# Own-phase keys of two attention groups in one 128-column segment, the division moved from the gate to the probabilities, and the value split regrouped

## The chip, the cores and the metric

The kernel runs on one core of one Trainium2 chip. The metric is the device time of one execution in microseconds (us). The engines are TensorE (PE, with its weight loads listed apart as PEld), VectorE (DVE), ScalarE (ACT), GpSimd (POOL) and SyncE (SP), which issues most of the transfers.

## The reference, cut to what matters

Two layers over 256 tokens of width 2048, in float32. Layer 0, where the change lies, is attention with three head groups of 16 heads each; a query of a group with dilation d attends to itself and to the tokens at multiples of d behind it, within a window.

```python
ATT_GROUPS = ((128, 1), (512, 4), (2048, 16))     # (window, dilation)
for g, (window, dilation) in enumerate(ATT_GROUPS):
    q = _head_rms(qkv[:, :, g, 0], q_gain[g]); k = _head_rms(qkv[:, :, g, 1], k_gain[g]); v = qkv[:, :, g, 2]
    o, lse = _dilated_window_attention(q, k, v, table, window, dilation)   # s = q.k/sqrt(128) + bias, softmax, p.v
w = jax.nn.softmax(jnp.stack(lses, axis=0), axis=0)
o = jnp.sum(w[..., None] * jnp.stack(outs, axis=0), axis=0)
y = o.reshape(B, S, ATT_WIDTH) * jax.nn.silu(z)
return y @ w_out
```

Weighing the three groups by their softmax denominators is the same as one softmax over the keys of all three. Layer 1 is a convolution module; the change doesn't touch it.

## The kernel before

**Tokens.** They are ordered by phase (token number modulo 4), 64 of each phase, in two blocks of 128 (`b`): block 0 holds phases 0 and 1, block 1 phases 2 and 3. Groups 1 and 2 (dilations 4 and 16) only ever look at keys of the query's own phase; group 0 looks at all.

**Precision.** Each float32 operand of a product is split into a high and a low part of a narrower format (`hi`, `lo`), and a product is three matmuls: high by high, low by high, high by low. The high part is a cast on ACT; the low part is a subtraction on DVE or POOL.

**The loop.** The program is one hand-ordered loop over 480 weight chunks of 512 KB. At step n PE multiplies chunk n (`project`: 12 matmuls of 512 columns), then chunk n+3 is fetched on SP's queue and split (`stage`: `hi` on ACT, `lo` on DVE, or on POOL in the output projection), and then the functions that `at(n, ...)` has put down for step n are written out. Those put down with `when=soon` come ahead of `stage`. Each engine runs its own instructions strictly in the order written. Steps 0 to 319 are the attention's input projection: eight sets of two heads, five column groups of eight steps each: (q,k) of groups 0, 1, 2, then the values of groups 0 and 1, then the values of group 2 with the gate `z`. The products of a column group lie in two of four PSUM banks (`acc`) that are used in turn. From step 320 comes the output projection (`wo`), which takes all four banks at once at its first step.

**A set's attention** runs among the steps of the next set, in four units (two heads by two token blocks): `scores` on PE, `softmax` (bias adds and maximum on DVE, exponential on ACT), `weigh` (reciprocal of the sum, which before scales the gate `zs`), `turn` (transposes of the probabilities on PE), `split` (high part on ACT, low on DVE). After both units of a head `values` runs on PE into bank `o`; `gated` and `y_split` make the output's parts. An ordinary set has three steps between units, the last set, whose attention runs among the output projection, two.

**What the steps touch.** Scores of a unit are 512 columns wide: 256 keys of group 0, then 128 keys of the query's block for each of groups 1 and 2, half of which are of the other phase and are masked by the bias. The bias is made at the start (`bias_rows`) in rows of eight segments of 128 per phase, held in DRAM (`btab`) and fetched per head. `v_split` (L359) splits the value banks, `z_take` (L374) copies the gate out of the last bank. `make_identity` gives `ident` for transposes; `r0` is the per-token norm, `r0h` half of it.

Of the kernel before, what the change touches and what calls it, by code (L numbers as in the profile page):

```python
# [11 lines left out]
F32 = mybir.dt.float32  # L12
F32R = mybir.dt.float32r
# [24 lines left out]
V_HEAD = V_BIN  # L38


@with_exitstack
def hybrid_kernel(ctx: ExitStack, tc: tile.TileContext, x_perm, x_tok, x_nat, vecs, rel, onehot, maskrow,
# [104 lines left out]
    xh = bpool.tile([P, KT, S], F32R, tag="xh", name="xh")  # L147
    xl = bpool.tile([P, KT, S], F32R, tag="xl", name="xl")
# [10 lines left out]
    r0 = cpool.tile([P, 2], F32, name="r0")  # L159
    r0h = cpool.tile([P, 2], F32, name="r0h")  # L160
# [3 lines left out]
    def x_split(k, xr):  # L164
        g0 = vec[:, V_G0 + k:V_G0 + k + 1]
        if k == 0:
            nc.vector.tensor_scalar(xh[:, k, :], xr, g0, None, op0=ALU.mult)
        else:
            nc.scalar.activation(xh[:, k, :], xr, AF.Copy, scale=g0)
        nc.vector.scalar_tensor_tensor(xl[:, k, :], xr, g0, xh[:, k, :].bitcast(F32), op0=ALU.mult, op1=ALU.subtract)  # L170
# [59 lines left out]


    btab = dram.tile([NH, 4096], F32, name="btab")
    brow = {}

    def bias_load(part):

        if part == 0:
            brow["rb"] = apool.tile([N_BUCKETS, NG * NH], F32, name="rb")
            nc.sync.dma_start(brow["rb"], rel)
            brow["oh"] = bpool.tile([N_BUCKETS, 4096], F32, tag="yl", name="oh")  # L240
            nc.sync.dma_start(brow["oh"], onehot)
        else:
            brow["row"] = bpool.tile([NH, 4096], F32, tag="yh", name="row")
            nc.sync.dma_start(brow["row"], bass.AP(tensor=maskrow.tensor, offset=maskrow.offset, ap=[[0, NH], [1, 4096]]))

    def bias_split(f):
        if f == 0:
            brow["hi"] = apool.tile([N_BUCKETS, NG * NH], F32R, name="rb_hi")
            brow["lo"] = apool.tile([N_BUCKETS, NG * NH], F32R, name="rb_lo")
            nc.scalar.copy(brow["hi"], brow["rb"])  # L250
            nc.vector.tensor_tensor(brow["lo"], brow["rb"], brow["hi"].bitcast(F32), op=ALU.subtract)
        brow["oh_r"] = apool.tile([N_BUCKETS, 1024], F32R, tag="pp", name=f"oh_r{f}", bufs=1)
        nc.scalar.copy(brow["oh_r"], brow["oh"][:, f * 1024:(f + 1) * 1024])

    def bias_rows(f, half):
        ps = t_tile(f"ps_b{f}_{half}")
        for g, c0, c1 in (((0, 0, 512),), ((1, 0, 256), (2, 256, 512)))[half]:
            for i, part in enumerate(("hi", "lo")):
                nc.tensor.matmul(ps[:NH, c0:c1], lhsT=brow[part][:, g * NH:(g + 1) * NH],
                                 rhs=brow["oh_r"][:, half * 512 + c0:half * 512 + c1], start=i == 0, stop=i == 1)  # L260
        row = brow["row"][:, f * 1024 + half * 512:f * 1024 + (half + 1) * 512]
        nc.vector.tensor_tensor(row, ps[:NH, :], row, op=ALU.add)

    def bias_store(f):
        sl = slice(f * 1024, (f + 1) * 1024)
        nc.scalar.dma_start(btab[:, sl], brow["row"][:, sl])

    for i in range(2):
        at(11 + i, bias_load, i)
# [8 lines left out]
    def load_bias(head):  # L278

        bt = apool.tile([P, 2, 512], F32, tag="bt", name=f"bt{head}", bufs=2)  # L280
        base = btab[:, :]
        for f in range(4):
            src = bass.AP(tensor=base.tensor, offset=base.offset + head * 4096 + f * 1024,
                          ap=[[1, 64], [128, 8], [1, 64]])
            p0 = (f % 2) * 64
            nc.sync.dma_start(bt[p0:p0 + 64, f // 2, :].rearrange("p (s i) -> p s i", s=8), src)
# [4 lines left out]
    def project(n):  # L291
# [9 lines left out]
        for i in range(2):  # L301
            k = kc * 2 + i
            wh, wl = hi[:, i * 512:(i + 1) * 512], lo[:, i * 512:(i + 1) * 512]
            for b, p in order:
                sl = slice(b * P, (b + 1) * P)
                nc.tensor.matmul(acc[b], lhsT=(xl if p == 1 else xh)[:, k, sl], rhs=wl if p == 2 else wh,  # L306
# [52 lines left out]
    def v_split(hs, part, width):  # L359
        acc = acc_a[hs * CG + 3 + part]  # L360
        out_ = []
# [641 lines left out]
```

## Time and profile before

| | |
|---|---|
| median of 3 runs | 1446.06 us (1444.73 to 1446.16) |
| the profiled execution, own time | 1443.28 us |
| its span, first to last instruction | 1441.5 us |
| PE busy | 1431.2 us, 99% |
| weight loads busy | 1186.3 us, 82% |
| DVE busy | 968.8 us, 67% |
| ACT busy | 720.3 us, 50% |
| POOL busy | 381.4 us, 26% |
| transfers | 272.09 MB, mean 189 GB/s |

Busy time is the union of an engine's instructions. Matmul records overlap: a 512-column matmul is listed with some 0.39 us, and the next starts 0.23 us after it, so on PE the distance from start to start is read. A row of the order of time gives the start, the length, the engine, the line, what is written and read, the shape, and in brackets idle time of the engine before it with what ended it.

### The profile page before, as it was taken

The page shows a single profiled execution, that of the slowest core. Times are in us where ns is not written, and L with a number is a line of the kernel's source. Part 1 is how long each engine was busy: PE and PEld are TensorE (multiplying, and loading weights), DVE is VectorE, ACT ScalarE, POOL GpSimd, SP SyncE. Part 2 cuts the span into 40 slices and gives each one's busy share as a digit, 9 for nine tenths or more (in the row PEclk, how much of TensorE's full clock was granted, in tenths as well). Part 3 has the DMA queues.
Part 4 walks back from the last instruction along what each step waited for, and adds up shares of the span by engine and source line. Part 5 has one row for each costly group of instructions (what it writes and reads, how often), then busy time and mean ns, then how long its engine had stood idle before and what let it go on. Part 6 is the DMA issues. An engine that isn't in the chain of part 4 may idle for free.

```text
span 1441.5 us, 18597 instructions
## 1 busy us (share of the span) xinstructions
PE 1431.2 (99%) x6730; PEld 1186.3 (82%) x6730; DVE 968.8 (67%) x1537; ACT 720.3 (50%) x999; POOL 381.4 (26%) x279
## 2 busy tenths in 40 slices
PE   9999999999999999999999999999999999999998
PEld 7778888888888888888888888888888888888777
DVE  6665765765676576576567657656668999988542
ACT  7544545454455454445445545544554445545642
POOL 0210120010011002001001100207104878787455
PEclk9999999999999999999999999999999999999999
DMA  9775558568557655755855765666665656665463
GB/s 353 234 196 193 157 176 220 160 174 218 169 165 193 197 166 178 208 171 165 220 172 163 194 199 162 179 170 235 193 208 183 185 179 191 177 192 171 146 205 132
DMA packets 108092, 272.09 MB, mean 189 GB/s; under 512 B 42224, under 2 KB 42736, under 8 KB 107824
## 3 DMA queue, kind: packets, MB, share of 16 engines
q1 hardware_dynamic: 107296, 270.23, 63.2%
q8 instruction: 53, 0.87, 0.3%
q10 hardware_dynamic: 704, 0.68, 0.2%
q14 instruction: 39, 0.32, 0.1%
HBM read 268.51 MB, written 2.36 MB: 188 GB/s over the span
## 4 chain that ended last, share of the span: by engine, by line
PE 95%; DVE 2%; ACT 1%; DMA 1%; issue 1%; POOL 1%; SPq 0%; DVEq 0%; ACTq 0%; POOLq 0%
PE acc L306 61%; PE b L536 6%; PE b L537 6%; PE b L538 6%; PE wo L536 2%; PE wo L538 2%; PE wo L537 2%; PE psq L343 1%; PE vo L538 1%; PE vo L536 1%; PE vo L537 1%; PE pt L430 1%; PE pg L697 1%; ACT hi L122 1%; PE o L457 1%
## 5 line engine op out<-in xcount | busy, mean ns | idle before, releaser
L122 ACT CAST hi<-raw 128x1024 fp32r<-128x1024 f32 x477 | 496.5, 1050 | 308.0 <-PE acc L306 177.0
L125 DVE TENSOR_TENSOR lo<-raw,hi 128x1024 fp32r<-128x1024 f32 x360 | 446.4, 1241 | 274.8 <-ACT hi L122 268.1
L306 PE MATMUL acc<-hi,xh 128*128 128x512 f32 x1280 | 505.4, 397 | 0.0
L306 PE MATMUL acc<-lo,xh 128*128 128x512 f32 x1280 | 497.3, 391 | 0.0
L306 PE MATMUL acc<-hi,xl 128*128 128x512 f32 x1280 | 495.6, 389 | 0.0
L125 POOL TENSOR_TENSOR lo<-raw,hi 128x1024 fp32r<-128x1024 f32 x117 | 283.6, 2459 | 151.4 <-ACT hi L122 98.5
L306 PEld LDWEIGHTS acc<-lo,xh 128*128 128x128 f32 x1280 | 240.0, 188 | 52.3 <-DVE lo L132 0.6
L306 PEld LDWEIGHTS acc<-hi,xh 128*128 128x128 f32 x1280 | 240.2, 188 | 49.2 <-issue 2.8
L306 PEld LDWEIGHTS acc<-hi,xl 128*128 128x128 f32 x1280 | 240.6, 188 | 47.0 <-DVE xl L170 0.4
L144 POOL TENSOR_SCALAR rq<-ss 128x4 f32<-128x4 f32 x48 | 10.3, 215 | 786.1 <-DVE ss L325 784.2
L750 DVE SCALAR_TENSOR_TENSOR c<-u,vec,c 128x256 f32<-128x256 f32 x480 | 190.5, 481 | 0.0
L536 PE MATMUL b<-hi,hh 128*128 128x512 f32 x384 | 151.0, 393 | 0.0
L538 PE MATMUL b<-lo,hh 128*128 128x512 f32 x384 | 149.7, 390 | 0.0
L537 PE MATMUL b<-hi,hl 128*128 128x512 f32 x384 | 149.5, 389 | 0.0
L538 PEld LDWEIGHTS b<-lo,hh 128*128 128x128 f32 x384 | 72.1, 188 | 15.1
L537 PEld LDWEIGHTS b<-hi,hl 128*128 128x128 f32 x384 | 72.2, 188 | 14.5
L536 PEld LDWEIGHTS b<-hi,hh 128*128 128x128 f32 x384 | 72.1, 188 | 14.4
L419 ACT ACTIVATE pr<-sc,m 128x512 f32<-128x512 f32 x32 | 23.2, 724 | 100.4 <-DVE m L417 100.4
L356 DVE TENSOR_TENSOR qk<-psq,qk 128x256 fp32r<-128x256 f32 x48 | 20.3, 422 | 51.1 <-ACT qk L355 51.1
L538 PE MATMUL vo<-lo,bh 128*128 128x512 f32 (+1 forms) x130 | 50.6, 389 | 1.5 <-POOL lo L125 1.5
L536 PE MATMUL wo<-hi,yh 128*128 128x512 f32 x128 | 51.3, 401 | 0.0
L536 PE MATMUL vo<-hi,bh 128*128 128x512 f32 (+1 forms) x130 | 50.4, 388 | 0.0
(145 smaller groups left out, 1299.2 us busy)
## 6 DMA issues: line engine op xcount, KB each, us to landing
raw<-w_in SPq DMA_DIRECT2D x319, 512.0 KB, 4.3
raw<-v_in SPq DMA_DIRECT2D x96, 512.0 KB, 4.3
raw<-w_out SPq DMA_DIRECT2D x32, 512.0 KB, 4.2
raw<-v_out SPq DMA_DIRECT2D x32, 512.0 KB, 4.3
bt<-btab SPq DMA_DIRECT2D x64, 128.0 KB, 6.0
x_tok<-x_tok SPq DMA_DIRECT2D x4, 512.0 KB, 8.5
x<-x_nat SPq DMA_DIRECT2D x4, 512.0 KB, 7.4
xr<-x_perm SPq DMA_DIRECT2D x7, 256.0 KB, 4.6
```

Of the source, the lines that this page charges most:

```text
L122: nc.scalar.copy(hi, raw)
L125: low_engine(n).tensor_tensor(lo, raw, hi.bitcast(F32), op=ALU.subtract)
L306: nc.tensor.matmul(acc[b], lhsT=(xl if p == 1 else xh)[:, k, sl], rhs=wl if p == 2 else wh, start=k == 0 and p == 0, stop=k == KT - 1 and ...
L343: nc.tensor.transpose(ps[:, c, :], qn[:, c, :], ident)
L356: nc.vector.tensor_tensor(ql, ps[:, 0:2], qh.bitcast(F32), op=ALU.subtract)
L419: nc.scalar.activation(u.pr.rearrange("p a b -> p (a b)"), sc, AF.Exp, bias=u.m[:, 1:2], accum_out=u.m[:, 2:3])
L430: nc.tensor.transpose(u.pt[:, c, :], u.pr[:, c, :], ident)
L457: nc.tensor.matmul(po[:, 2 * b * P:2 * (b + 1) * P], lhsT=vh[:, cs], rhs=pp[:, 2 + i, 2 * b:2 * b + 2, :], start=False, stop=False, skip_g ...
L536: nc.tensor.matmul(acc, lhsT=xh_, rhs=wh, start=first, stop=False, skip_group_check=part)
L537: nc.tensor.matmul(acc, lhsT=xl_, rhs=wh, start=False, stop=False, skip_group_check=part)
L538: nc.tensor.matmul(acc, lhsT=xh_, rhs=wl, start=False, stop=last, skip_group_check=part)
L750: nc.vector.scalar_tensor_tensor(c[j], u, w, c[j], op0=ALU.mult, op1=ALU.add)
```

## The change

Own-phase keys of groups 1 and 2 now share one 128-column segment: for a query of phase f, 64 columns of one group and 64 of the other, so a unit's scores are 384 columns wide and no own-phase column is masked for phase. The score matmuls stay as they were; the four halves are picked out of their result by DVE adds of 64 partitions by 64 columns. Which group comes first in the segment depends on the phase.

- `turn` transposes three blocks of 128 and no longer four; `split` takes 384 columns.
- `values`: the own-phase products have 128 and 64 moving columns instead of 256 and 128. Their weights `w` hold 64 tokens of one group and 64 of the other, so that `v_split` writes them in halves of 64 partitions. For this the fifth column group (values of group 2, and the gate) is projected with the tokens turned by 64: `xh` and `xl` get 64 tokens more at their end (`turn_norm`, two POOL copies), `rs` holds the norms in turned order (five small transfers), and `z_turn` and `z_put` turn the gate back, with two copies.
- `split_scaled` writes the high parts of a bank (ACT) ahead of its low parts (DVE).
- `weigh` multiplies the probabilities by the reciprocal on ACT; the gate isn't scaled any more.
- In the last set `v_split` and `z_take` of the last bank pair come ahead of `stage` (`when=soon`).
- The bias: 33 rows by 3072 columns, with a 33rd row for the masked places in place of a mask row that was added; the bias tiles have 384 columns.

```diff
+    def turn_norm():
+
+        nc.sync.dma_start(rs[:64], rr[64:])
+        for c in range(4):
+            nc.sync.dma_start(rs[64:, c:c + 1], rr[:64, c ^ 1:(c ^ 1) + 1])
+        for x in (xh, xl):
+            nc.gpsimd.tensor_copy(x[:, :, S:], x[:, :, :64])
+
+    at(20, turn_norm)
...
     def bias_rows(f, half):
         ps = t_tile(f"ps_b{f}_{half}")
-        for g, c0, c1 in (((0, 0, 512),), ((1, 0, 256), (2, 256, 512)))[half]:
+        h0 = half * 512
+        pieces = [(0, 0, 512)] if half == 0 else [(1 + f % 2, 0, P), (2 - f % 2, P, 2 * P)]
+        for g, c0, c1 in pieces:
             for i, part in enumerate(("hi", "lo")):
                 nc.tensor.matmul(ps[:NH, c0:c1], lhsT=brow[part][:, g * NH:(g + 1) * NH],
-                                 rhs=brow["oh_r"][:, half * 512 + c0:half * 512 + c1], start=i == 0, stop=i == 1)
...
+                t0 = b * P + 64 * (cg % CG == 4)
+                tokens = (xl if p == 1 else xh)[:, k, t0:t0 + P]
+                nc.tensor.matmul(acc[b], lhsT=tokens, rhs=wl if p == 2 else wh,
...
+    def split_scaled(pieces):
+
+        for hi, lo, src, r in pieces:
+            nc.scalar.activation(hi, src, AF.Copy, scale=r)
+        for hi, lo, src, r in pieces:
+            nc.vector.scalar_tensor_tensor(lo, src, r, hi.bitcast(F32), op0=ALU.mult, op1=ALU.subtract)
+
+    def v_split(hs, part):
...
+        for b in range(2):
+            pieces = []
+            if part == 0:
+                pieces.append((*sets[hs].v0[b], acc[b][:, :S], r0[:, b:b + 1]))
+            c0, r = ((S, r0), (0, rs))[part]
+            for i in range(2):
+                ps = slice(i * 64, (i + 1) * 64)
+                w = sets[hs].w[b ^ (part & i)]
+                pieces.append((*[x[ps, i ^ part, :] for x in w], acc[b][ps, c0:c0 + S], r[ps, b:b + 1]))
+            split_scaled(pieces)
...
+        for g in range(2):
+            for p in range(2):
+                ps, c = slice(p * 64, (p + 1) * 64), p ^ g
+                nc.vector.tensor_tensor(s6[ps, 4 + c], u.py[ps, g, 0, ps], bias[ps, 4 + c], op=ALU.add)
+                nc.vector.tensor_tensor(s6[ps, 4 + c], s6[ps, 4 + c], u.py[ps, g, 1, ps], op=ALU.add)
...
         nc.vector.reciprocal(u.m[:, 3:4], u.m[:, 2:3])
-        zs = u.set.zs[u.b][:, u.h * P:(u.h + 1) * P]
-        nc.vector.tensor_scalar(zs, zs, u.m[:, 3:4], None, op0=ALU.mult)
+        nc.scalar.activation(u.pr, u.pr, AF.Copy, scale=u.m[:, 3:4])
...
-        for c in range(4):
+        for c in range(3):
             nc.tensor.transpose(u.pt[:, c, :], u.pr[:, c, :], ident)
...
+            wh, wl = st.w[b]
+            for f_ in range(2):
+                qs = slice(f_ * 64, (f_ + 1) * 64)
+                nc.tensor.matmul(po4[:, 2 * b:2 * b + 2, f_, :], lhsT=wh[:, f_, cs], rhs=pp[:, 2, 2 * b:2 * b + 2, qs],
                                  start=False, stop=False, skip_group_check=True)
-                nc.tensor.matmul(po[:, q0:q0 + P], lhsT=vl[:, cs], rhs=pp[:, 2 + i, 1 + b, :],
-                                 start=False, stop=i == 1, skip_group_check=True)
+                nc.tensor.matmul(po4[:, 1 + b, f_, :], lhsT=wl[:, f_, cs], rhs=pp[:, 2, 1 + b, qs],
+                                 start=False, stop=True, skip_group_check=True)
...
-        at(e + 1 - last, v_split, hs, 1, 256)
-        at(e + 1 - last, z_take, hs)
+        at(e + 1 - last, v_split, hs, 1, when=soon if last else steps)
+        at(e + 1 - last, z_take, hs, when=soon if last else steps)
```

How the change moves instructions stands at three places. In the rows below a name is that of the tile written, then `<-` and the tiles read, then the shape written; a number at a name's end tells buffers apart.

ACT, between the last step of the input projection and the first exponential of the last set, before (`vh`: high values of a bank, `zs`: the gate):

```order
L365 ACTIVATE vh_1_0_8407<-acc_0_8243,r_82 128x256
L365 ACTIVATE vh_1_1_8411<-acc_1_8244,r_82 128x256
L379 ACTIVATE zs_0_8415<-acc_0_8243,r0h 128x256
L379 ACTIVATE zs_1_8417<-acc_1_8244,r0h 128x256
L122 CAST hi_8436<-raw_8435 128x1024
L122 CAST hi_8464<-raw_8463 128x1024
L419 ACTIVATE pr_0_8475,m_0_8470<-sc_0_8469,m_0_8470 128x512
```

The same place now (`wh`: high values in halves of 64 partitions):

```order
L378 ACTIVATE wh_0_8509<-acc_0_8487,rs 64x256
L378 ACTIVATE wh_1_8513<-acc_0_8487,rs 64x256
L378 ACTIVATE wh_1_8513<-acc_1_8488,rs 64x256
L378 ACTIVATE wh_0_8509<-acc_1_8488,rs 64x256
L407 ACTIVATE zs_0_8665<-acc_0_8487,rs 128x256
L407 ACTIVATE zs_1_8667<-acc_1_8488,rs 128x256
L123 CAST hi_8670<-raw_8669 128x1024
L123 CAST hi_8692<-raw_8691 128x1024
L123 CAST hi_8720<-raw_8719 128x1024
L448 ACTIVATE pr_0_8737,m_0_8726<-sc_0_8725,m_0_8726 128x384
```

Two high parts stand ahead of the gate copies instead of one per bank, and one more cast (that of chunk 322, which stood ahead of this place) stands behind them.

DVE, the same place up to the first unit's gate scaling, before (`vl`: low values, `sc`: scores with bias, `m`: maximum, sum and reciprocal):

```order
L366 SCALAR_TENSOR_TENSOR vl_1_0_8408<-acc_0_8243,r_82,vh_1_0_8407 128x256
L366 SCALAR_TENSOR_TENSOR vl_1_1_8412<-acc_1_8244,r_82,vh_1_1_8411 128x256
L412 TENSOR_TENSOR sc_0_8469<-s_0_8441,bt_8307 128x256
L413 TENSOR_TENSOR sc_0_8469<-sy_0_8442,bt_8307 128x256
L416 TENSOR_TENSOR sc_0_8469<-sc_0_8469,sy_0_8442 128x256
L417 TENSOR_REDUCE m_0_8470<-sc_0_8469 128x1
L387 SCALAR_TENSOR_TENSOR zs_0_8415<-e_0_8496,zs_0_8415 128x256
L423 RECIPROCAL m_0_8470<-m_0_8470 128x1
L425 TENSOR_SCALAR zs_0_8415<-zs_0_8415,m_0_8470 128x128
```

The same place now, where the pair L444, L445 stands four times in all:

```order
L380 SCALAR_TENSOR_TENSOR wl_0_8510<-acc_0_8487,rs,wh_0_8509 64x256
L380 SCALAR_TENSOR_TENSOR wl_1_8514<-acc_0_8487,rs,wh_1_8513 64x256
L380 SCALAR_TENSOR_TENSOR wl_1_8514<-acc_1_8488,rs,wh_1_8513 64x256
L380 SCALAR_TENSOR_TENSOR wl_0_8510<-acc_1_8488,rs,wh_0_8509 64x256
L126 TENSOR_TENSOR lo_8671<-raw_8669,hi_8670 128x1024
L439 TENSOR_TENSOR sc_0_8725<-s_0_8697,bt_8563 128x256
L444 TENSOR_TENSOR sc_0_8725<-sy_0_8698,bt_8563 64x64
L445 TENSOR_TENSOR sc_0_8725<-sc_0_8725,sy_0_8698 64x64
...
L446 TENSOR_REDUCE m_0_8726<-sc_0_8725 128x1
L415 SCALAR_TENSOR_TENSOR zs_0_8665<-e_0_8758,zs_0_8665 128x256
L452 RECIPROCAL m_0_8726<-m_0_8726 128x1
```

Four low parts and the subtraction of chunk 322 now stand ahead of the first adds, eight small adds stand in place of two, and the scaling of the gate behind the reciprocal is gone.

PE, in the values of a head (`o`: the output bank, `pp`: probabilities), the end of the all-phase products and the beginning of the own-phase ones, before:

```order
L451 MATMUL o_1_8784<-pp_2_8706,vl_0_1_8268 128x256
L457 MATMUL o_1_8784<-pp_2_8706,vh_0_0_8263 128x256
L459 MATMUL o_1_8784<-pp_2_8706,vl_0_0_8264 128x128
L457 MATMUL o_1_8784<-pp_2_8706,vh_1_0_8407 128x256
L459 MATMUL o_1_8784<-pp_2_8706,vl_1_0_8408 128x128
```

The same place now:

```order
L479 MATMUL o_1_9061<-pp_2_8983,v0l_1_8512 128x256
L485 MATMUL o_1_9061<-pp_2_8983,wh_0_8509 128x2x64
L487 MATMUL o_1_9061<-pp_2_8983,wl_0_8510 128x64
...
L485 MATMUL o_1_9061<-pp_2_8983,wh_1_8513 128x2x64
L487 MATMUL o_1_9061<-pp_2_8983,wl_1_8514 128x64
```

The eight own-phase matmuls stay eight, with half as many moving columns each.

## Rows read from the trace of the kernel before

**Rows 1.** The page, busy time by engine: us, share of the span, instructions.

```profile
PE 1431.2 (99%) x6730; PEld 1186.3 (82%) x6730; DVE 968.8 (67%) x1537; ACT 720.3 (50%) x999; POOL 381.4 (26%) x279
```

**Rows 2.** Order of time on PE around one `turn`: start us, length us, instruction.

```profile
293.15 0.60 PE L430 MATMUL pt<-ident,pr 128*128 128x128 f32 x4
...
293.82 0.40 PE L306 MATMUL acc<-hi,xl 128*128 128x512 f32 x1
294.05 0.40 PE L306 MATMUL acc<-lo,xh 128*128 128x512 f32 x1
```

**Rows 3.** Order of time on PE in one block of the bias rows.

```profile
60.27 0.28 PE L259 MATMUL ps_b<-oh_r,rb_lo 32*16 32x256 f32 x1
60.39 0.27 PE L259 MATMUL ps_b<-oh_r,rb_hi 32*16 32x256 f32 x1
```

**Rows 4.** Order of time on PE, own-phase values of one head.

```profile
300.48 0.28 PE L457 MATMUL o<-pp,vh 128*128 128x256 f32 x1
300.59 0.22 PE L459 MATMUL o<-pp,vl 128*128 128x128 f32 x1
300.65 0.33 PE L457 MATMUL o<-pp,vh 128*128 128x256 f32 x1
...
301.34 0.45 PE L306 MATMUL acc<-hi,xh 128*128 128x512 f32 x1
```

**Rows 5.** Order of time on PE, token sums with one moving column.

```profile
1328.05 0.95 PE L215 MATMUL ps_ln<-ones,sb 128*128 128x1 f32 x8
1328.87 0.48 PE L536 MATMUL b<-hi,hh 128*128 128x512 f32 x1
```

**Rows 6.** Order of time on DVE, second unit of an ordinary set.

```profile
265.05 0.42 DVE L416 TENSOR_TENSOR sc<-sc,sy 128x256 f32<-128x256 f32 x1
265.51 0.69 DVE L417 TENSOR_REDUCE m<-sc 128x1 f32<-128x512 f32 x1
...
269.15 0.16 DVE L423 RECIPROCAL m<-m 128x1 f32<-128x1 f32 x1
```

**Rows 7.** Order of time on PE, the transposes of that unit.

```profile
271.88 0.60 PE L430 MATMUL pt<-ident,pr 128*128 128x128 f32 x4
```

**Rows 8.** Order of time on ACT, end of the input projection.

```profile
968.42 0.47 ACT L365 ACTIVATE vh<-acc,r 128x256 fp32r<-128x256 f32 x1 [3.93 <-PE acc L306]
969.10 0.47 ACT L365 ACTIVATE vh<-acc,r 128x256 fp32r<-128x256 f32 x1 [0.20 <-PE acc L306]
969.48 0.47 ACT L379 ACTIVATE zs<-acc,r0h 128x256 f32<-128x256 f32 x1
970.13 0.47 ACT L379 ACTIVATE zs<-acc,r0h 128x256 f32<-128x256 f32 x1 [0.19 <-DVE vl L366]
```

**Rows 9.** Order of time on PE there, first use of the freed banks.

```profile
970.26 0.39 PE L536 MATMUL wo<-hi,yh 128*128 128x512 f32 x1
```

**Rows 10.** The page, costliest groups: casts and subtractions of weights.

```profile
L122 ACT CAST hi<-raw 128x1024 fp32r<-128x1024 f32 x477 | 496.5, 1050 | 308.0 <-PE acc L306 177.0
L125 DVE TENSOR_TENSOR lo<-raw,hi 128x1024 fp32r<-128x1024 f32 x360 | 446.4, 1241 | 274.8 <-ACT hi L122 268.1
...
L125 POOL TENSOR_TENSOR lo<-raw,hi 128x1024 fp32r<-128x1024 f32 x117 | 283.6, 2459 | 151.4 <-ACT hi L122 98.5
```

**Rows 11.** Order of time on DVE, first two units of the last set.

```profile
972.18 0.42 DVE L412 TENSOR_TENSOR sc<-s,bt 128x256 f32<-128x256 f32 x1 [2.08 <-PE s L399]
...
979.68 2.23 DVE L425 TENSOR_SCALAR zs<-zs,m 128x128 f32<-128x128 f32 x1
...
988.23 0.15 DVE L423 RECIPROCAL m<-m 128x1 f32<-128x1 f32 x1
```

**Rows 12.** Order of time on PE in the last set.

```profile
988.30 0.60 PE L430 MATMUL pt<-ident,pr 128*128 128x128 f32 x4
...
995.59 0.50 PE L450 MATMUL o<-pp,vh 128*128 128x512 f32 x1 [0.24 <-DVE pp L439]
```

More of the change, by code (lines that the diff above doesn't have):

```diff
@@ L249, in bias_split @@
-            brow["lo"] = apool.tile([N_BUCKETS, NG * NH], F32R, name="rb_lo")
+            brow["row"] = bpool.tile([NH, 4 * ROW], F32, tag="yh", name="row")
+            parts = apool.tile([N_BUCKETS + 1, 2, NG * NH], F32R, tag="xs", name="rb_r", bufs=1)
+            brow["hi"], brow["lo"] = parts[:, 0], parts[:, 1]
             nc.scalar.copy(brow["hi"], brow["rb"])
             nc.vector.tensor_tensor(brow["lo"], brow["rb"], brow["hi"].bitcast(F32), op=ALU.subtract)
-        brow["oh_r"] = apool.tile([N_BUCKETS, 1024], F32R, tag="pp", name=f"oh_r{f}", bufs=1)
@@ L258, in bias_rows @@
+        for g, c0, c1 in pieces:
             for i, part in enumerate(("hi", "lo")):
                 nc.tensor.matmul(ps[:NH, c0:c1], lhsT=brow[part][:, g * NH:(g + 1) * NH],
-                                 rhs=brow["oh_r"][:, half * 512 + c0:half * 512 + c1], start=i == 0, stop=i == 1)
-        row = brow["row"][:, f * 1024 + half * 512:f * 1024 + (half + 1) * 512]
-        nc.vector.tensor_tensor(row, ps[:NH, :], row, op=ALU.add)
+                                 rhs=brow["oh_r"][:, h0 + c0:h0 + c1], start=i == 0, stop=i == 1)
@@ L264, in bias_store @@
+        width = pieces[-1][2]
+        c0 = f * ROW + h0
+        nc.vector.tensor_copy(brow["row"][:, c0:c0 + width], ps[:NH, :width])
     def bias_store(f):
-        sl = slice(f * 1024, (f + 1) * 1024)
+        sl = slice(f * ROW, (f + 1) * ROW)
         nc.scalar.dma_start(btab[:, sl], brow["row"][:, sl])
-    for i in range(2):
-        at(11 + i, bias_load, i)
+    at(11, bias_load)
     for f, e in enumerate((17, 21, 23, 25)):
@@ L930, in _bias_constants @@
 def _bias_constants():
-    onehot = np.zeros((N_BUCKETS, 4, 8, 128), np.float32)
-    mask = np.full((4, 8, 128), NEG, np.float32)
+    onehot = np.zeros((N_BUCKETS + 1, 4, 6, 128), np.float32)
     for f in range(4):
-        for s in range(8):
-            g = 0 if s < 4 else 1 if s < 6 else 2
-            fk = s if s < 4 else 2 * (f // 2) + s % 2
+        for s in range(6):
+            g = 0 if s < 4 else 1 + (s + f) % 2
+            fk = s if s < 4 else f
             dil, win = DILATION[g], WINDOW[g]
-            for j in range(127):
+            for j in range(128):
                 dist = 4 * (j - 63) + f - fk
-                if dist >= 0 and dist % dil == 0 and dist <= win:
-                    mask[f, s, j] = 0.0
+                if j < 127 and dist >= 0 and dist % dil == 0 and dist <= win:
                     onehot[int(_bucket(np.array(dist))), f, s, j] = 1.0
-    return onehot.reshape(N_BUCKETS, 4096), mask.reshape(1, 4096)
+                else:
+                    onehot[N_BUCKETS, f, s, j] = 1.0
+    return onehot.reshape(N_BUCKETS + 1, 4 * ROW)
 def _groups(w):
```

111 lines of the change are left out of this document (47 added, 64 removed).

## Prediction, made before the changed kernel was run

> **What bounds the kernel now.** I read the share of busy time first: TensorE (PE) has a matmul under way for 1431.2 of 1441.5 us [rows 1]. So a term counts in full if it shortens what PE does, and for nothing if it lies on VectorE (DVE), ScalarE (ACT), GpSimd (POOL) or the DMA queues, unless PE comes to wait there. Matmuls overlap in the records, so busy time is no price; I read the price of a matmul from the distance between starts in PE's order of time. A full 512-column matmul takes 0.23 us (293.82 to 294.05) [rows 2]. Then I looked, for each place where the change makes another engine later, at how long before PE's need it is done now.
>
> **PE's savings.** (1) *One transpose less in each of 32 units.* A block of four transposes (L430) runs from 293.15; the second matmul after it starts at 293.82, and one matmul of 0.23 lies between: 0.44 us, or 0.11 each [rows 2]. The same block stands in every unit, so 32 x 0.11 = **3.5 us**.
>
> (2) *Bias rows.* In each of four blocks the four 256-column matmuls become 128-column ones. Two 256-column ones start 0.12 apart [rows 3]. For 128 columns the bounds are 0.06 (what such a matmul takes in the values, 300.59 to 300.65 [rows 4]) and 0.11 (a transpose); so 16 x (0.12 - 0.06) = 1.0 or 16 x 0.01 = 0.2. Here the weights have only 16 columns, so I stand near the first: **0.8 us**.
>
> (3) *Own-phase values.* Each of 16 heads has eight matmuls, 256 and 128 columns in turn, which become 128 and 64. This looks like the largest saving and is, I think, nearly nothing. The eight run from 300.48 to 301.34: 0.86 us, 0.108 each [rows 4]. By columns they would take about 4 x (0.12 + 0.06) = 0.72. What sets the pace is the loading of weights: eight matmuls with a single moving column (L215) start at 1328.05 and are followed at 1328.87: 0.82 us, 0.103 each [rows 5]. The change keeps eight loads of 128 columns. Between 0.103 and 0.108 each, a head gains 0 to 0.04, 16 heads 0 to 0.6; I take **0.3 us**.
>
> Of the Trainium skill, "TensorE: Matmul & The Clock Gate", section "Back-to-back issue gap", speaks against this: it gives about 81 ns per load-and-matmul pair at 128 columns in a sustained stream, by which, as an estimate, the eight would take 0.65 us, 16 heads would gain 3.4 us, and the sum below would be some 3 us larger. No row here shows loads of 128 columns closer than 0.10 us.
>
> **What is added, and what hides it.** In seven of eight sets the unit chain is: scores, adds and maximum on DVE, exponential on ACT, reciprocal on DVE, then (new) the division on ACT, and the transposes. In the tightest unit of a set the reciprocal starts at 269.15 and ends by 269.31, and PE's transposes start at 271.88 [rows 6, 7]: 2.57 us of slack. Into it go: the 128x384 division on ACT, at most 0.6 (a 256-column pass took 0.47 [rows 8]); and the longer adds. Two 256-column adds of about 0.46 each become eight 64x64 adds. A DVE operation took 0.42 for 256 columns and 0.16 for one [rows 6], so 0.22 for 64; each second add waits for the first, as 265.05 to 265.51 shows (0.04 more than its length). Eight cost 1.6 us if pairs overlap, 2.1 if none does, less 0.9 removed and 0.13 for the shorter maximum: +0.6 to +1.1. So 2.57 - 0.6 - 1.1 = 0.9 us is left at worst, and PE sees nothing. The split of values (ten passes on ACT and ten on DVE for four and four), the POOL copy of 64 tokens and the five small transfers on SP at step 20 stand eight or more projection steps (2.7 us each: 12 x 0.23) ahead of what reads them. SP, where weight loads queue behind these transfers, waits there for a POOL result of step 11. Fewer bias descriptors and a missing mask load take load off the DMA queues, on which PE doesn't wait.
>
> "VectorE: DVE Perf Modes", section "Two Vector instructions with no wait between them", of the Trainium skill says that an instruction whose operand starts in another quadrant of partitions is held until all earlier ones have finished. The new adds change halves three times per unit; by it the dearer end (2.1 us) holds. No row of before alternates halves, so none shows it.
>
> **The last set is another matter**, because the output projection follows with no spare bank. PE takes up the two banks of the last column group at 970.26 and, three matmuls of 0.23 on, 970.95 [rows 9]; ACT now frees them at 969.95 and 970.60, after one high part and one gate copy per bank [rows 8]. After the change ACT makes two high parts per bank, 0.38 apart; DVE's first low part waits for both (968.42 + 0.38 + 0.47 = 969.27), two low parts follow, for which I take 0.47 each too, and only then the gate copy: done at 970.7 for the first bank; for the second 971.45 if DVE's passes overlap, 971.85 if not. PE then waits 0.45 and 0.05 us, or 0.55 and 0.35: 0.5 to 0.9, I take **0.7 us lost**.
>
> Next, the second unit's reciprocal ends at 988.38, 0.08 *after* its transposes began at 988.30 [rows 11, 12]; today nothing depends on it, then it does. Also the cast and the subtraction of chunk 322, 1.05 and 1.24 us [rows 10], now stand behind the value split: from the last gate copy's end, 971.45 to 971.85, they put the first adds at 973.7 to 974.1 instead of 972.18 [rows 11], some 1.0 later once PE's own wait of 0.7 is taken off. Two softmaxes add 1.2 to 2.2, of which 0.2 comes back in narrower passes. In return the gate scaling L425 leaves DVE: 2.23 us here, for 128 columns, which I put down to the subtractions that POOL runs meanwhile [rows 11]. Net for the reciprocal: 1.0 + 1.0 - 2.2 = -0.2, to +0.8; with 0.08 and the division's 0.6 the transposes would wait 0.5 to 1.5 us. Where the gate product L387, ahead of the reciprocal and as exposed to POOL, now falls into a pause of POOL, up to two of these microseconds come back. I take **0.4 us lost**, bounds 0 and 1.5. On the other side PE waits 0.24 us for low probabilities at 995.59 [rows 12]; DVE reaches them without two scalings, so **0.2 us gained**.
>
> Sum: 3.5 + 0.8 + 0.3 + 0.2 - 0.7 - 0.4 = 3.7 us. The profiled execution took 1443.28 us, so it would take 1439.6; the three runs' median lies 2.8 us higher, nothing in the change touches what lies around the span, and I take the 3.7 off the median: **1442.4 us**.
>
> **Rivals.** *A, columns pay after all.* If 128 and 64 columns take 0.06 and 0.03, a head's eight take 0.36 instead of 0.86, 16 heads gain 8 us: about 1434; by half of it 1438. For it: 128 columns pass in 0.06 behind a 256-column matmul [rows 4]. Against: the single-column rows at 0.103 [rows 5]. Chance 0.05. The Trainium skill's pace per pair, quoted above from "TensorE: Matmul & The Clock Gate", would land here.
>
> *B, POOL's quantum.* In the last set a gate product on DVE that just misses a gap between POOL subtractions ends a whole operation later, 2.46 us [rows 10], and the reciprocal and division behind it now hold PE. One such miss makes the second unit's transposes wait 2.4 more: 1444.8, no measurable difference. For it: the 2.23 in rows 11; against: ACT feeds POOL in the same order as DVE, with gaps. Chance 0.22.
>
> *C, slower.* The 64x64 adds cost far more than 0.26. The tight unit has 2.57 - 0.6 + 0.13 + 0.9 = 3.0 us for eight, so from 0.38 each PE waits at its transposes in every set. At 0.5 each that is 1.0 us in seven sets and about 1.5 more in the last: 8.5 lost, 1451. Rows 6 speak against it (0.42 for four times the columns). Chance 0.05.
>
> **How the numbers follow.** The forecast spans 1441.3 (savings 0.8 larger, no wait at the second transposes, 0.5 at the banks) to 1444.6 (all small terms at their bad ends at once), mostly 1441.3 to 1443.6, and has a chance of 0.68. A measurement can tell about 0.2% (2.9 us) from no change, so a gain counts below 1443.2: most of the forecast (0.61) and A are faster: 0.66. The forecast's upper edge and B are the same: 0.29. C is slower: 0.05. For 8 in 10 the range takes in the forecast and B: 1440.4 to 1445.2.
>
> **What would show it.** In the changed profile: blocks of three transposes 0.33 long; own-phase matmuls still 0.11 apart (0.06 would be A); bias matmuls near 0.06; a first wait of PE for ACT's gate copy at the start of the output projection, 0.3 to 1 us; DVE's eight adds 1.6 to 2.1 us in all; in sets 1 to 7 no wait before transposes. I'm wrong if PE waits for ACT's division in ordinary sets, or if the last set's waits add up to more than 2 us.

## The result, and the profile after

The changed kernel takes 1461.21 us (median of 4 runs, 1460.17 to 1461.77) against 1445.88 us for the kernel before (4 runs, 1444.73 to 1446.16): a ratio of 1.0112, 95% interval 1.01 to 1.0124. It is slower, by 15 us between the medians and 16 by the ratio. The prediction, 1442.4 us with a range of 1440.4 to 1445.2, was wrong, and on the wrong side. The profiled execution has a span of 1459.9 us, 18.4 more than before; that is some 3 us more than the medians differ, since the execution of before that was profiled is a short one (2.6 us below its median).

Two lines of the page of the changed kernel: busy time by engine (it answers to [rows 1]), and the engines' shares of the chain that ended last, of which PE had 95% before.

```profile
PE 1434.1 (98%) x6698; PEld 1181.9 (81%) x6698; DVE 991.4 (68%) x1745; ACT 744.4 (51%) x1095; POOL 383.5 (26%) x282
...
PE 71%; DVE 12%; issue 8%; ACT 6%; DMA 1%; POOL 1%; ACTq 0%; DVEq 0%; SPq 0%; POOLq 0%
```

PE has fewer instructions and is now idle for 25.8 of the 1459.9 us; before it was 10.3 of 1441.5. The waits of PE in the changed kernel, summed by line and by what ended them (us in all, times, longest), and then those of the kernel before:

```profile
PE psq L359 <- DVE pp L467: 7.7, 7, 1.1
PE pt L458 <- ACT pr L453: 5.4, 8, 0.8
PE pg L727 <- ACT gate L898: 3.1, 1, 3.1
PE pz L512 <- DVE pp L467: 2.4, 7, 0.3
PE ps_warm L212 <- POOL ident masks.py:199: 1.4, 1, 1.4
PE vo L568 <- POOL lo L126: 0.9, 1, 0.9
PE wo L566 <- ACT zs L407: 0.5, 1, 0.5
...
```

```profile
PE pg L697 <- ACT gate L868: 3.1, 1, 3.1
PE vo L538 <- POOL lo L125: 1.5, 3, 0.6
PE ps_warm L208 <- POOL ident masks.py:199: 1.4, 1, 1.4
PE o L450 <- DVE pp L439: 0.2, 1, 0.2
```

Three are new and come once in each of the seven ordinary sets: the next set's normed columns (`psq`) and the gate's transposes (`pz`), which want a bank from which DVE is still taking the low part of the probabilities (`pp`), and the transposes (`pt`) behind ACT's division. A set, measured from the first value matmul of one to that of the next, is 123.12 us long in the mean of six, against 120.61 before: 2.5 us more, where by the prediction's terms (3.5 + 0.3 over eight sets) 0.5 less was to come. Over the span: six set lengths +15.0 (738.70 against 723.68 us), from there to the output projection +2.1, its stretch with the last set +0.4, the parts before and behind +0.9, 18.4 in all. So the loss lies in the ordinary sets, not in the last one, on which the prediction spent most of its care.

**Where a unit's time goes.** The chain of waits of the changed kernel between the maxima of the third and the fourth unit of one set (start us, us, what; a set has four units, two heads by two token blocks):

```profile
280.80 0.56 DVE m L446
...
281.38 0.71 ACT pr L448 x2
282.09 0.95 ACT hi L123
...
283.13 1.07 issue
284.20 0.17 DVE m L452
...
284.45 0.62 ACT pr L453
285.07 0.95 ACT hi L123
...
286.05 1.23 DVE lo L126
287.27 0.34 DVE y L495
...
289.73 0.46 DVE pp L467
290.20 0.33 DVE sc L439
...
292.41 0.56 DVE m L446
```

There is no PE in it: ACT and DVE hand work back and forth. Maximum (DVE), exponential (ACT), cast of the next weights (ACT), their subtraction (DVE; the 1.07 "issue" is most of it), the reciprocal, which stands behind that subtraction in DVE's order, the division (ACT), the next cast, which stands behind the division (ACT), its subtraction (DVE), the parts of the last head's output, the low probabilities and the adds (DVE), and the next maximum. From maximum to maximum it is 11.6 us, and the round before it (269.20 to 280.80) is 11.6 too. I call such a closed round of hand-overs the ring. Before, units followed PE's pace: the transposes of the second and the fourth unit lie 21.27 us apart (271.88 to 293.15), 10.6 a unit. A set has three rounds, and then its units pause until the next set: 10.4, 11.6 and 11.6 us here, 10.2, 9.5 and 11.4 before (maxima at 255.27, 265.51, 274.97 and 286.36). One long round alone therefore says little; it is the sum of the three that has grown, from 31.1 to 33.6 us. ACT's order of time in the changed kernel shows the hand-over; the bracket is idle time:

```profile
270.40 1.03 ACT L123 CAST hi<-raw 128x1024 fp32r<-128x1024 f32 x1
272.86 0.62 ACT L453 ACTIVATE pr<-pr,m 128x384 f32<-128x384 f32 x1 [1.43 <-DVE m L452]
```

### The profile page after: what moved, and what is told of

Read it like the earlier page. It is cut to its first block, busy times and chain, and to the rows that moved or that the text cites. A ratio compares the mean times of both kernels' runs of the same rounds, so it can differ in the third digit from the quotient of the medians.

```text
span 1459.9 us, 18839 instructions
## 1 busy us (share of the span) xinstructions
PE 1434.1 (98%) x6698; PEld 1181.9 (81%) x6698; DVE 991.4 (68%) x1745; ACT 744.4 (51%) x1095; POOL 383.5 (26%) x282
## 4 chain that ended last, share of the span: by engine, by line
PE 71%; DVE 12%; issue 8%; ACT 6%; DMA 1%; POOL 1%; ACTq 0%; DVEq 0%; SPq 0%; POOLq 0%
PE acc L322 42%; PE b L566 6%; PE b L568 6%; PE b L567 6%; ACT hi L123 4%; DVE lo L126 4%; DVE sc L445 2%; DVE sc L444 2%; PE wo L566 2%; PE wo L568 2%; PE wo L567 2%; PE psq L359 1%; POOL lo L126 1%; DVE m L446 1%; ACT pr L448 1%
## 5 line engine op out<-in xcount | busy, mean ns | idle before, releaser
L448 ACT ACTIVATE pr<-sc,m 128x384 f32<-128x384 f32 x32 | 19.7, 617 | 128.7 <-DVE m L446 128.7
L370 ACT CAST qk<-psq 128x256 fp32r<-128x256 f32 x48 | 17.8, 372 | 69.3 <-PE psq L359 69.3
```

The source lines that it names most:

```text
L370: nc.scalar.copy(qh, ps[:, 0:2])
L448: nc.scalar.activation(u.pr.rearrange("p a b -> p (a b)"), sc, AF.Exp, bias=u.m[:, 1:2], accum_out=u.m[:, 2:3])
```

## The experiments

Three batches of kernels, each with the kernel before timed beside them (medians 1444.72, 1444.96 and 1444.67 us). The first asks which of the two additions in an ordinary unit costs the time, ACT's division or DVE's eight adds, by undoing one at a time or doing one alone.

**Division on DVE** (the changed kernel, ACT's share undone):

```diff
-        nc.scalar.activation(u.pr, u.pr, AF.Copy, scale=u.m[:, 3:4])
+        nc.vector.tensor_scalar(u.pr, u.pr, u.m[:, 3:4], None, op0=ALU.mult)
```

> The changed kernel took 1461.2 us; PE waits about 18.6 us in sets 1 to 7 (0.5, 0.9 and 1.3 us per set). Here the division of the probabilities is done by VectorE right behind the reciprocal (a 128x384 tensor_scalar) instead of by ScalarE; nothing else differs. Theory W (ScalarE stands idle at the division until VectorE has made a weight subtraction and the reciprocal, so its next cast and VectorE's next subtraction come late, and with them the low probabilities): the waits of PE in sets 1 to 7 go to under 3 us in total, time 1443 to 1446 us. Rival V (the eight small adds on VectorE, some 1.0 us more per unit, make the low probabilities late): VectorE has 0.3 us more per unit still, so the waits stay or grow: 1459 to 1465 us.

**Division early** (the changed kernel; `weigh`, so reciprocal and division, written ahead of the weights' split of its step):

```diff
-                at(t + dt, fn, u)
+                at(t + dt, fn, u, when=soon if fn == weigh else steps)
```

> The division stays on ScalarE, but reciprocal and division are put ahead of the staging of the step's weight chunk (when=soon), so that the reciprocal no longer stands behind a weight subtraction on VectorE and the division not behind a cast. Theory W: ScalarE's wait at the division falls from 1.1 to 1.4 us per unit to about 0.3, waits of PE in sets 1 to 7 fall to under 4 us in total, time 1443 to 1448 us. Rival V: the adds are as long as before, the waits stay: 1457 to 1462 us.

**Four adds** (the changed kernel; one add takes both columns' halves, 64 partitions by 128):

```diff
-        for g in range(2):
-            for p in range(2):
-                ps, c = slice(p * 64, (p + 1) * 64), p ^ g
-                nc.vector.tensor_tensor(s6[ps, 4 + c], u.py[ps, g, 0, ps], bias[ps, 4 + c], op=ALU.add)
-                nc.vector.tensor_tensor(s6[ps, 4 + c], s6[ps, 4 + c], u.py[ps, g, 1, ps], op=ALU.add)
+        for p in range(2):
+            ps = slice(p * 64, (p + 1) * 64)
+            y = u.py[ps, ::-1] if p else u.py[ps]
+            nc.vector.tensor_tensor(s6[ps, 4:], y[:, :, 0, ps], bias[ps, 4:], op=ALU.add)
+            nc.vector.tensor_tensor(s6[ps, 4:], s6[ps, 4:], y[:, :, 1, ps], op=ALU.add)
```

> The eight 64x64 adds of a unit become four of 64x128 (both groups of a half at once, same values). VectorE's adds fall from 1.97 to about 1.2 us per unit. Theory W: the units get 0.8 us earlier but ScalarE's wait at the division stays, so of the 18.6 us of waits in sets 1 to 7 perhaps a third goes: 1453 to 1458 us. Rival V: most of the waits go: 1443 to 1449 us.

**The division alone in the kernel before:**

```diff
-        zs = u.set.zs[u.b][:, u.h * P:(u.h + 1) * P]
-        nc.vector.tensor_scalar(zs, zs, u.m[:, 3:4], None, op0=ALU.mult)
+        nc.scalar.activation(u.pr, u.pr, AF.Copy, scale=u.m[:, 3:4])
```

> The kernel before, with one part of the change alone: the reciprocal no longer scales the gate on VectorE, ScalarE multiplies the probabilities (128x512) instead. Theory W: ScalarE waits at the division as in the changed kernel, and PE waits 1 to 2.5 us per set at the transposes that follow: 1453 to 1465 us. Rival V (adds): the unit chain has no longer adds and PE sees next to nothing: 1445 to 1449 us.

Measured: division on DVE 1446.79 us (ratio to before 1.0013, 1.0003 to 1.0022), division early 1445.79 (1.0007, 0.9997 to 1.0017), four adds 1442.31 (0.9982, 0.9973 to 0.9992), the division alone 1445.35 (1.0001, 0.9992 to 1.001). Division early lies in the range that I had given theory W, the division alone in that of V; division on DVE is 0.8 us above W's, the four adds 0.7 below V's. Undoing either addition brings the time to within some 2 us of before, or below it; the division alone costs nothing that can be measured. So neither is the cause by itself, and both theories as I had stated them fall. What was left was a joint cause. I first placed it in the bank: before, DVE's low part of the last unit is done 1.49 us before PE takes the bank for the next set, as these rows of the kernel before show (DVE, then PE):

```profile
294.40 0.69 DVE L439 TENSOR_TENSOR pp<-pt,pp 128x512 fp32r<-128x512 f32 x1 [0.85 <-ACT pp L438]
```

```profile
296.58 0.60 PE L343 MATMUL psq<-ident,qn 128*128 128x128 f32 x4
```

(294.40 and 0.69 make 295.09.) In the changed kernel that low part begins at 300.77 and PE waits:

```profile
301.38 0.65 PE L359 MATMUL psq<-ident,qn 128*128 128x128 f32 x4 [1.09 <-DVE pp L467]
```

The second batch tested the joint cause from the other side, built it up in the kernel before, and asked whether the bank is what matters.

**Eight adds alone in the kernel before** (eight of 128 partitions by 64 columns, so halves of columns and not of partitions; they replace the two of 256 columns, whose lines are left out here):

```diff
+        for g in range(2):
+            for p in range(2):
+                c, s = slice(p * 64, (p + 1) * 64), 4 + 2 * g + p
+                nc.vector.tensor_tensor(s8[:, s], u.py[:, g, 0, c], bias[:, s], op=ALU.add)
+                nc.vector.tensor_tensor(s8[:, s], s8[:, s], u.py[:, g, 1, c], op=ALU.add)
```

> The kernel before with one edit: the two subtractions and additions of VectorE over 256 columns are made as eight over 64 columns, with the same data and no other change (the segments, the gate factor and the order of the values stay). Theory J (joint): VectorE has 1.48 us between the low part of the probabilities of the last unit and TensorE's next use of that bank; the eight cost between 0.65 and 1.06 us more than the two, which fits, so about 1445 to 1447 us. Rival V (the eight instructions alone bring the loss): 1452 us or more. If each next add overlapped with the one before (its operands lie on other partitions or columns), pitches of about 0.17 to 0.2 us; if none overlaps, about 0.24 us each, as in the changed kernel.

**Eight adds and the division in the kernel before** (the two diffs above together):

> As f1, and the probabilities divided by ScalarE, with the gate unscaled. Theory J: the late reciprocal (about 0.6 us behind ScalarE's division) and the eight adds (0.65 to 1.06 us) together exceed the 1.48 us, and TensorE waits in each of the seven ordinary sets: 1455 to 1462 us. Rival (the shared segment or the order of the value parts is needed for the loss): 1449 us or less.

**The low probabilities early** (the changed kernel; `split` written ahead of the weights' split):

```diff
-                at(t + dt, fn, u)
+                at(t + dt, fn, u, when=soon if fn == split else steps)
```

> The changed kernel, with the two parts of the transposed probabilities issued ahead of VectorE's and ScalarE's other waiting work, so that the bank comes free earlier; the eight adds and the late division stay. Theory J, in which the loss is made of TensorE waiting for that bank: the waits of z's turn and of the next set's scores vanish, about 1445 to 1451 us. Rival (the late division itself holds up the transposes and the values, whatever the bank does): 1455 us or more.

**Four adds and the division early** (two diffs of the first batch together):

> The changed kernel with both causes lessened: four adds over 64 partitions and 128 columns in place of the eight, and the subtraction of the weights that stands ahead of the reciprocal given way to it. Theory J: no wait of TensorE for VectorE in the seven ordinary sets, what is gained is the shorter work of TensorE less some of the last set's loss, 1440 to 1442.5 us, faster than both kernels. Rival (either alone already gave all there is): no better than the four adds alone, 1442.3 us or more.

Measured: eight adds alone 1446.79 (1.0014, 1.0004 to 1.0023), nearly nothing; eight adds and the division 1464.17 (1.0137, 1.0121 to 1.0153). That is 2 us above the range that I had expected. So the two make the whole loss in the kernel before, without the shared segment, the turned tokens, the new order of the value parts, or the single buffer that the output tile `y` has in the changed kernel (two before). The low probabilities early: 1461.99 (1.0121, 1.0105 to 1.0137), no help. My expectation (1445 to 1451) failed, and the waits say how. With the bank free, the set is as long as ever (123.07 us), and PE waits for the division instead, twice per set and in all 13.1 us:

```profile
PE pt L458 <- ACT pr L453: 13.1, 15, 1.6
```

So the bank is only where the loss surfaces; freeing it left the maxima of the units 11.6 us apart (270.45, 282.04 and 293.65 in the chain of that kernel). That is the ring. Four adds and the division early: 1440.7 (9 runs; 0.9975, 0.9965 to 0.9985), faster than both kernels. None of the three new waits is left:

```profile
PE pg L727 <- ACT gate L898: 3.1, 1, 3.1
PE ps_warm L212 <- POOL ident masks.py:199: 1.4, 1, 1.4
PE wo L566 <- ACT zs L407: 0.5, 1, 0.5
PE acc L322 <- ACT xh L173: 0.2, 1, 0.2
PE vo L568 <- POOL lo L126: 0.2, 1, 0.2
```

How the early reciprocal opens the ring is seen in ACT's idle time before all 32 divisions (us, times), in the changed kernel and then in this one:

```profile
  DVE m L452: 44.0, 32
```

```profile
  DVE m L452: 7.4, 32
```

The third batch tested the ring by its length: in steps, by work of another kind, and with the order changed but the adds kept.

**Both early, eight adds kept** (the changed kernel):

```diff
-                at(t + dt, fn, u)
+                at(t + dt, fn, u, when=soon if fn in (weigh, split) else steps)
```

> The changed kernel, eight adds kept, with both the subtraction of the weights given way to the reciprocal and the two parts of the transposed probabilities issued ahead. Ring theory (in a unit ScalarE and VectorE hand work to each other in a closed ring of 11.6 us, longer than TensorE's own pace; the early reciprocal takes the ring apart, and what the early division alone left is the late low part of the last unit): the rest of the waits goes, 1441 to 1443 us, below the kernel before. Rival (VectorE with eight adds is itself too slow for TensorE's pace, whatever the order): 1445 us or more, as with the early division alone.

**The division and four adds in the kernel before** (128 partitions by 128 columns each, in place of the two; the removed lines and the division, as above, are left out):

```diff
+        for g in range(2):
+            s = slice(4 + 2 * g, 6 + 2 * g)
+            y = u.py[:, g].rearrange("p c (s i) -> p c s i", s=2)
+            nc.vector.tensor_tensor(s8[:, s], y[:, 0], bias[:, s], op=ALU.add)
+            nc.vector.tensor_tensor(s8[:, s], s8[:, s], y[:, 1], op=ALU.add)
```

> The kernel before with ScalarE's division and four adds of 128 partitions and 128 columns, between the two adds (no loss measured) and the eight (19 us lost). Ring theory: the adds take about 1.2 us, between 0.9 and 1.56, the ring is some 0.3 us shorter than with eight, and the loss comes in between, as three rings in a set: 1450 to 1458 us. Rival (a threshold, something that happens or does not): no loss, below 1448 us, or the whole of it, above 1460 us.

**Eight adds and two unused maxima in the kernel before, no division** (added to the diff with the eight adds alone):

```diff
+        for _ in range(2):
+            nc.vector.tensor_reduce(u.m[:, 0:1], sc, op=ALU.max, axis=AX.X, negate=True)
```

> The kernel before with the eight adds and without any division by ScalarE, and two more maxima over the scores (0.70 us each, their results not used) ahead of the one that counts. The ring is then 1.4 us longer than with the eight adds alone, about as long as with eight adds and the division or longer. Ring theory (only its length counts): TensorE waits in every ordinary set, 1462 to 1472 us. Rival (the division's own place on ScalarE, behind a reciprocal that waits for a cast, is needed): 1452 us or less.

Measured: both early 1449.5 (1.0031, 1.002 to 1.0043); the division and four adds 1450.89 (1.0041, 1.0026 to 1.0056), in between as expected; the unused maxima 1476.37 (1.022, 1.0203 to 1.0237), 4 us more than expected. The last run has no division on ACT, no shared segment and no ACT work that wasn't there before; a longer VectorE share of a unit alone makes PE wait in every set at two of the three places, at one of them for another low part (`qk`). Its waits there:

```profile
PE psq L343 <- DVE pp L441: 8.6, 7, 1.2
PE pz L486 <- DVE qk L357: 7.9, 7, 1.1
```

Part of what it takes beyond the expectation is PE's clock and not the waits themselves. In its profile the granted clock falls from full speed (2.4 GHz) to half (1.2 GHz) four times, for 3.4 us each, from 428, 800, 1022 and 1387 us on; the first three come within 3 us behind two waits of PE of 0.8 to 1.2 us. Two of the six sets hold such a fall and last 125.2 us, the other four 123.6: 1.6 us for each fall. By that, as an estimate, the four falls cost some 6.5 us. All four runs of this kernel have a mean clock of 0.995, the runs of the changed kernel 0.999.

Both early failed: expected 1441 to 1443, measured 7 us more, and 4 more than the division early alone. The bank is then free in time, but the normed columns' low parts (`qk`) stand further back on DVE, and the gate's transposes wait for them:

```profile
PE pz L512 <- DVE qk L373: 5.1, 7, 0.7
```

The time lies in the range of the rival set beside it, by which DVE with eight adds is too slow whatever the order. The division on DVE speaks against that rival: there DVE has the eight adds and the division too, and PE waits for nothing in the ordinary sets.

All kernels side by side. The pace is the distance from the second unit's last maximum to the fourth's in one set (two units), from DVE's order of time; the set length is a mean of six. With three blocks of transposes a set without waits is 120.29 us (the two kernels that reach it), with four 120.61; the last column but one is what lies above that.

| kernel | adds, division | pace, us | set, us | above | median, us |
|---|---|---|---|---|---|
| before | 2, gate scaled | 20.86 | 120.61 | 0 | 1444.7 to 1445.9 |
| four adds, division early | 4, ACT early | 21.11 | 120.29 | 0 | 1440.7 |
| before + eight adds | 8, gate scaled | 21.54 | 120.61 | 0 | 1446.8 |
| four adds | 4, ACT | 21.80 | 120.47 | 0.18 | 1442.3 |
| division on DVE | 8, DVE | 21.89 | 120.29 | 0 | 1446.8 |
| before + division | 2, ACT | 21.93 | 120.85 | 0.24 | 1445.4 |
| before + division + four adds | 4, ACT | 22.45 | 121.63 | 1.02 | 1450.9 |
| division early | 8, ACT early | 22.52 | 120.90 | 0.61 | 1445.8 |
| both early | 8, ACT early | 22.52 | 121.40 | 1.11 | 1449.5 |
| low probabilities early | 8, ACT | 23.19 | 123.07 | 2.78 | 1462.0 |
| **changed** | 8, ACT | 23.21 | 123.12 | 2.83 | 1461.2 |
| before + eight adds + division | 8, ACT | 23.46 | 123.40 | 2.79 | 1464.2 |
| before + eight adds + maxima | 8, gate scaled | 24.18 | 124.17 | 3.56 | 1476.4 |

Up to 21.9 us for two units a set loses at most 0.24; from 22.45 it loses 0.6 to 1.1, from 23.2 nearly 3 (3.0 in the last row's four sets without a fall of the clock). PE's own distance between the transposes of these units is 21.27 before and 21.09 in the best kernel. So DVE and ACT may take PE's pace and less than a microsecond more; from there on PE waits.

Division on DVE stands out: its ordinary sets have no waits, although DVE keeps the eight adds and gets the division on top. ACT no longer stops for the reciprocal and casts on, so the next subtraction finds its weights ready: behind the reciprocals of one set's first two units DVE idles 1.7 us before it in the changed kernel (to 264.05 and 274.45) and not at all here (259.41 and 269.31). One hand-over less counts for more than the longer work. The loss of this kernel sits in the last set, where PE waits for the division twice; the second wait is followed by a fall of the clock to half (991.5 to 994.9 us):

```profile
PE pt L458 <- DVE pr L453: 4.1, 2, 2.9
```

```profile
L453 DVE TENSOR_SCALAR pr<-pr,m x32: 420/421/2340, 138.8 to 1003.6; 128x384 f32<-128x384 f32 x32
```

(min, median and longest ns of the 32.) The four long ones, of 1.6 to 2.3 us, each ran while a POOL subtraction was under way. That is the kind of stall that the prediction's rival B names, made real by this edit.

## Why the prediction was wrong, point by point

**PE's savings: right, somewhat small.** (1) Blocks of three transposes: 0.98 us per set in the order of time of the kernel whose waits are gone, where four took 1.42; 0.44 saved per set and 3.5 over eight, as predicted. Less of it arrives: a set without waits is only 0.32 us shorter (120.29 against 120.61), the own-phase values included, since its 512-column matmuls take 0.2 us more in all. No run here shows why. (2) Bias rows: four 128-column matmuls take 0.34 us up to the next matmul, against 0.57 for the four before (60.14 to 60.71), 0.23 a block and 0.9 over four blocks; 0.8 was taken. (3) Own-phase values stay bound by the loading of weights: from 305.32 to 306.14 is 0.82 us for eight, 0.103 each, where 0.86 [rows 4] was before and 0.82 to 0.86 was forecast. PE in the changed kernel:

```profile
60.95 0.41 PE L273 MATMUL ps_b<-oh_r,rb_r 33*16 33x128 f32 x4
61.29 0.50 PE L322 MATMUL acc<-hi,xh 128*128 128x512 f32 x1
...
305.32 0.23 PE L485 MATMUL o<-pp,wh 128*128 128x128 f32 x1
305.39 0.24 PE L487 MATMUL o<-pp,wl 128*128 128x64 f32 x1
...
306.14 0.48 PE L322 MATMUL acc<-hi,xh 128*128 128x512 f32 x1
```

Rival A is out. The Trainium skill, "TensorE: Matmul & The Clock Gate", section "Back-to-back issue gap", gives about 81 ns for a pair of load and matmul at 128 columns; the trace here has 103 for these, half of which have only 64 columns, and the measurement decides. In the kernel whose waits are gone, all savings with the last set's losses come to 1441.5 - 1438.2 = 3.3 us of span and 4.3 us between medians; the sum had 3.7.

**"PE sees nothing": this is the step that failed.** The sizes that went into it hold. The eight adds take 1.97 us from the first start to the maximum's (278.83 to 280.80), between the 1.6 and 2.1 forecast and near the dear end, 1.06 more than before; the division takes 0.62. And the slack of the second unit came out as I had it, 0.76 us between the division's end (273.48) and the transposes (274.24), where 0.9 was to be left. What failed is what I took this slack for. I measured it at one unit, called that the tightest, and let the next unit start from nothing. But what delays a unit's division delays ACT's next cast, so DVE's next subtraction, so the adds of the next unit, which stand behind it. The lateness is handed on: the maxima of the four units lie at 258.8, 269.2, 280.8 and 292.4 us, and at the fourth the transposes wait 0.76 us for the division although that unit had more slack before (2.98 us, 290.17 to 293.15) than the second (2.57). Nor did I price ACT's waiting: the division costs ACT not 0.6 but 2.0 us, the 1.38 it idles before each for a reciprocal (44.0 / 32) included. In the kernel before nothing on ACT queued behind the reciprocal, so this hand-over was no part of the round. And I looked at PE's need for the transposes only, not at its other meeting point with this work, the bank: its slack was 1.49 us, less than the 1.7 I was spending. [rows 6, 7] could not show either; a row of the third and fourth units, and of the next user of the bank, would have.

The experiments show this in each direction: taking either addition out of the ring gives all or most back, putting both into the old kernel makes the loss, a longer ring without a division makes it too, and freeing the bank alone does nothing. What isn't settled is the size within the last two microseconds: kernels of the same pace (division early, both early) differ by 0.5 us per set. Which low part stands behind which on DVE differs between them; that this makes the difference is argued and not tested.

**The last set: right in sum, partly by luck.** At the two banks of the last column group PE waits for the gate copies, and at the second unit's transposes for the division; the stall at the values [rows 12] is gone:

```profile
988.42 0.50 PE L566 MATMUL wo<-hi,yh 128*128 128x512 f32 x1 [0.53 <-ACT zs L407]
...
988.99 0.40 PE L568 MATMUL wo<-lo,yh 128*128 128x512 f32 x1
989.44 0.50 PE L566 MATMUL wo<-hi,yh 128*128 128x512 f32 x1
...
1007.16 0.55 PE L458 MATMUL pt<-ident,pr 128*128 128x128 f32 x3 [0.18 <-ACT pr L453]
...
1013.66 0.40 PE L568 MATMUL wo<-lo,yh 128*128 128x512 f32 x1
1013.89 0.39 PE L478 MATMUL o<-pp,v0h 128*128 128x512 f32 x1
```

By distances the first bank costs 0.68 us (987.51 to 988.42 instead of 0.23) and the second 0.22 more (988.99 to 989.44), 0.9 in all, where 0.7 was taken for the two. The transposes cost 0.34 (1006.59 to 1007.16) where 0.4 was taken, and the stall that is gone had cost 0.4 (994.96 to 995.59 before) where 0.2 was, so that the errors of two terms cancel. The whole stretch is 0.4 us longer than before (100.10 against 99.70 us from the first matmul of the output projection to the first of the next): 0.9 and 0.34 lost, less this 0.4 and the 0.44 that four shorter blocks of transposes save.

**The rivals.** B did not come about in the changed kernel: the transposes that it would have held for 2.4 us more waited 0.34. C, the slower one, had the right place, a DVE share of the unit that grows too long, and the wrong account: it let adds of at most 0.26 us pass and asked for 0.38 each. Measured, they are 0.25 apart and the loss came all the same, since C counted against the same one unit's slack. The case that took place, both additions within one ring, was among neither forecast nor rivals; with it the slower side deserved far more than 0.05.

## What to carry to other kernels

Where two engines hand work to each other, follow one round of it, from an operation to the same operation of the next unit through everything queued in between, and compare its length with the bounding engine's pace; slack at one unit does not show it. An operation that waits for a result of the other engine costs its own engine the wait as well, and everything behind it, so before moving one across, look at what is queued in front of the result it waits for. And list every place where the bounding engine meets this work, buffers that it reuses included, with the slack of each.

## What the runs showed of the hardware that was not expected

In these kernels DVE's short adds overlap where the partitions stay the same, and not where they change from one half to the other. With 64 partitions in turn (the changed kernel), each starts 0.23 to 0.26 us after the last, whether it needs its result or not; with 128 partitions (eight adds in the kernel before), the one that needs nothing starts 0.13 or 0.14 after it, and eight take 1.67 us instead of 1.97. DVE's order of time, changed kernel first:

```profile
278.83 0.20 DVE L444 TENSOR_TENSOR sc<-sy,bt 64x64 f32<-64x64 f32 x1
279.07 0.21 DVE L445 TENSOR_TENSOR sc<-sc,sy 64x64 f32<-64x64 f32 x1
279.30 0.23 DVE L444 TENSOR_TENSOR sc<-sy,bt 64x64 f32<-64x64 f32 x1
```

```profile
264.96 0.21 DVE L415 TENSOR_TENSOR sc<-sy,bt 128x64 f32<-128x64 f32 x1
265.21 0.22 DVE L416 TENSOR_TENSOR sc<-sc,sy 128x64 f32<-128x64 f32 x1
265.35 0.21 DVE L415 TENSOR_TENSOR sc<-sy,bt 128x64 f32<-128x64 f32 x1
```

This is what the Trainium skill, "VectorE: DVE Perf Modes", section "Two Vector instructions with no wait between them", says of an operand in another quadrant of partitions, and these rows agree. A 128x384 multiplication on DVE, 0.42 us as a rule, took up to 2.34 us in the stretch where POOL makes its subtractions. And PE's granted clock fell to half (1.2 GHz) for 3.4 us at a time, often just behind a wait of PE but not behind each: the 3.1 us wait for the gate (`pg`) comes once in every kernel, and such a fall follows it within 1 us in the changed kernel (1374.0 to 1377.4) but not in the kernel before.
